# Preparing a seven-product pair's weights beside the two chunks in front of it, with the plain blocks' high parts in a tile of the large pool

## Chip, cores and metric

The kernel runs on one core of a Trainium2 chip. The metric is the device time of one execution in microseconds; before the change the median of three runs is 1595.82 us (1594.87 to 1597.53).

## What is computed

One decoder layer over 256 tokens of width 2048, all in float32:

```python
u = rmsnorm(h, g_mix);  proj = u @ w_in                    # q, k, v, z, xBC, dt, two gates
out_a = attention(q, k, v) @ w_attn_br                      # sliding window, sinks
out_s = rmsnorm(ssd(xBC, dt) * silu(z), g_ssd) @ w_ssd_br   # state-space mixer
h = h + (sigmoid(g_a) * out_a + sigmoid(g_s) * out_s) @ w_o
f = rmsnorm(h, g_ffn)
h = h + (silu(f @ w_gate) * (f @ w_up)) @ w_down            # hidden width 5632
h = h + sigmoid(rmsnorm(h, g_ple) @ w_ple_gate) * (p @ w_ple_proj)
out = rmsnorm(h, g_final)
```

Nearly all of the time goes into products of 256 tokens with weight matrices that are read once from HBM.

## The kernel before

**Products.** A float32 matrix is split into a high part (a cast to float32r) and a low part (what the cast left). A product is three matmuls: high with high, high with low, low with high, each of 128 rows, 128 tokens and 512 columns. For weights, ScalarE (ACT) makes the high part `wh` from the loaded tile `wr`, and VectorE (DVE) makes the low part `wl` as `wr - wh`.

**Wide blocks.** `wide_block` computes 256 tokens by two column halves (q = 0, 1) of 512. It walks over pairs `kp` of 128-row slices of the weights. A plain pair is two chunks, one for each column half: a chunk is one load of 512 KB on SyncE's (SP's) queue (L298), one cast (L309), one subtraction (L311) and 4 products, that is 12 matmuls, written at L249. The last products of one pair are followed by the first of the next; only TensorE's (PE's) sums in PSUM link them.

**Seven-product pairs.** For the pairs named in `forms` a scheme of Strassen's kind makes 7 products (21 matmuls) of what would be 8 (24). It needs the two loads `raw[0]`, `raw[1]`, four additions of weight blocks into `tr` (L329; each 128x512, the last two each need the one ahead), and splits (L337 on ACT, L338 on DVE) of three plain blocks, b11 and b21 (one 128x1024 cast and subtraction) and b22 (128x512), and of `tr` (128x2048, parts `th` and `tl`). Products are taken in the order q1 (b11), c11 (b21), c12 (b22), q6, q7, q5, c21 (the four sums). There are 40 such pairs: 22 in the eleven blocks of `hidden` (the gate and up weights; pairs 2 and 5 of eight), 10 with `w_down`, 4 with the gate of the second branch, 2 with `w_ssd_br`, 2 with `w_o`. Two of them are never neighbours.

**Buffers.** `wr` has 4 buffers, `wh` 4, `wl` 3; the pool `big` has 17 buffers of 8 KB per partition for everything large. A `wl` tile is free again when PE has done the chunk that reads it. A seven-product pair takes 2 of `wr`, 2 of `wh`, 2 of `wl` (one for b22 alone) and 3 of `big` (`tr`, `th`, `tl`).

**Order.** Every engine executes its instructions in an order fixed when the kernel is built. The tile framework draws it up: among the instructions that it holds to be ready, the one that stands first in the source goes first, so the source's order is a preference and not the order itself. Work of other stages (transposes, normalisation sums) waits in a queue, of which `pump` writes out one or two items after each chunk.

Around a block's start DVE also has the end of the block before: `settle` (L361), the gated product (L1062) in `hidden`, or `add_settled` (L365, L367), and the splits of transposed activations (L133, L139).

Of the kernel before, what the change touches and what calls it, by code (L numbers as in the profile page):

```python
# [11 lines left out]
F32 = mybir.dt.float32  # L12
F32R = mybir.dt.float32r
I32 = mybir.dt.int32
AF = mybir.ActivationFunctionType
ALU = mybir.AluOpType
AX = mybir.AxisListType

P = 128
# [4 lines left out]
NB = 512  # L24
# [37 lines left out]
def block_kernel(ctx: ExitStack, tc: tile.TileContext, x, x_t, p_t, positions, vecs, rows, g_final,  # L62
                 w_in, w_attn_br, w_ssd_br, w_o, w_gate, w_up, w_down, w_ple_gate,
                 w_ple_proj, out):
    nc = tc.nc
# [3 lines left out]
    wraw_p = ctx.enter_context(tc.tile_pool(name="wraw", bufs=4))  # L69
    whi_p = ctx.enter_context(tc.tile_pool(name="whi", bufs=4))  # L70
    wlo_p = ctx.enter_context(tc.tile_pool(name="wlo", bufs=3))
# [5 lines left out]
    def big(shape, dtype=F32, name="big"):  # L77
        return big_p.tile(shape, dtype, name=name, tag="big")
# [18 lines left out]
    def pump(n):  # L97
        for _ in range(n):
            for q in (side, heads):
                if q:  # L100
                    q.popleft()()
# [57 lines left out]
    def stat(tiles, k):  # L159
        return tiles[k // 4][:, 0, k % 4, :], tiles[k // 4][:, 1, k % 4, :]  # L160
# [120 lines left out]
    def wide_block(halves, lhs, nk, forms, pumps=1):  # L281

        psum.reverse()
        np_, ns = nk // 2, len(forms)  # L290
        c11, c12, c21, c22 = sums = [
            Sums(acc_tile, 2 * (np_ - ns) + (ns if i < 3 else 0)) for i in range(4)]
        shared, done = None, 0
        parts = [None] * 4

        def load(q, kp, dst):
            w, col0 = halves[q]
            nc.sync.dma_start(out=dst, in_=w[2 * kp * P:2 * (kp + 1) * P, col0:col0 + NB].rearrange(  # L298
                "(k p) n -> p k n", p=P))

        for kp in range(np_):
            ev, od = lhs(2 * kp), lhs(2 * kp + 1)
            tok = [[[x[:, t * P:(t + 1) * P] for x in k] for k in (ev, od)] for t in range(NT)]
            if kp not in forms:
                for q in range(2):
                    wr = wraw_p.tile([P, 2, NB], F32, name="wr", tag="wr")
                    load(q, kp, wr)
                    wh = whi_p.tile([P, 2, NB], F32R, name="wh", tag="wh")
                    nc.scalar.copy(out=wh, in_=wr)  # L309
                    wl = wlo_p.tile([P, 2, NB], F32R, name="wl", tag="wl")  # L310
                    nc.vector.tensor_tensor(out=wl, in0=wr, in1=wh.bitcast(F32), op=ALU.subtract)  # L311
                    for k in range(2):
                        for t in range(NT):
                            sums[2 * t + q].add(tok[t][k], (wh[:, k], wl[:, k]))
                    pump(pumps)
                continue
            if shared is None:
                shared = [Sums(aux_tile, ns) for _ in range(4)]
            q1, q5, q6, q7 = shared
            a, g2, f3, s3 = [[forms[kp][:, i, 0], forms[kp][:, i, 1]] for i in range(4)]  # L320
            raw = [wraw_p.tile([P, 2, NB], F32, name="wr", tag="wr") for _ in range(2)]
            for q in range(2):
                load(q, kp, raw[q])
            tr = big([P, 4, NB], F32, name="tr")
            for o, x, y in ((tr[:, 0], raw[0][:, 0], raw[1][:, 0]),
                            (tr[:, 1], raw[1][:, 0], raw[1][:, 1]),
                            (tr[:, 2], tr[:, 1], raw[0][:, 0]),
                            (tr[:, 3], tr[:, 2], raw[0][:, 1])):
                nc.vector.tensor_tensor(out=o, in0=x, in1=y, op=ALU.add)  # L329
            split = []  # L330
            for x, xh, xl in (
                    (raw[0], whi_p.tile([P, 2, NB], F32R, name="wh", tag="wh"),
                     wlo_p.tile([P, 2, NB], F32R, name="wl", tag="wl")),
                    (raw[1][:, 1:2], whi_p.tile([P, 2, NB], F32R, name="wh", tag="wh")[:, 1:2],
                     wlo_p.tile([P, 2, NB], F32R, name="wl", tag="wl")[:, 1:2]),
                    (tr, big([P, 4, NB], F32R, name="th"), big([P, 4, NB], F32R, name="tl"))):
                nc.scalar.copy(out=xh, in_=x)  # L337
                nc.vector.tensor_tensor(out=xl, in0=x, in1=xh.bitcast(F32), op=ALU.subtract)  # L338
                split.extend((xh[:, i], xl[:, i]) for i in range(x.shape[1]))
            b11, b21, b22, t1, t3, t2, t4 = split  # L340
            q1.add(tok[0][0], b11)
            c11.add(tok[0][1], b21)
            c12.add(f3, b22)
            q6.add(g2, t2)
            q7.add(s3, t3)
            q5.add(a, t1)
            c21.add(tok[1][1], t4)
            pump(2 * pumps)
            done += 1
            if done == ns:  # L350
                mid = big([P, 4, NB], F32, name="mid")
                parts = [mid[:, i] for i in range(4)]
                nc.scalar.copy(out=parts[0], in_=q1.tile)
                for o, x, y, op in ((3, 0, q6, ALU.subtract), (2, 3, q7, ALU.add),
                                    (1, 3, q5, ALU.add), (3, 2, q5, ALU.add)):
                    nc.vector.tensor_tensor(out=parts[o], in0=parts[x], in1=y.tile, op=op)
        return [x.tile for x in sums], parts
# [248 lines left out]
    for t in range(NT):  # L606
        nc.vector.scalar_tensor_tensor(out=dtv[:, t], in0=accs[1][t][:, W2 - SSM_H:W2],
                                       scalar=r1[:, t:t + 1],
                                       in1=row[:, R_DTB:R_DTB + SSM_H],
# [354 lines left out]
    def cols(j):  # L964
        return slice(j * NB, (j + 1) * NB)
# [19 lines left out]
    for j in range(4):  # L985
        accs = nblock(w_attn_br, j * NB, lambda k: stat(attnT, k), 8)
        for t in range(NT):
            nc.vector.tensor_tensor(out=merged[t][:, cols(j)], in0=accs[0][t],
                                    in1=merged[t][:, cols(j)], op=ALU.mult)
# [17 lines left out]
    for jj in range(2):  # L1007
        sums, parts = wide_block(column_pair(w_in, GSO, jj), lhs_u, KD, uforms)
        for i in range(4):
            settle(i, sums, parts)  # L1010
            nc.scalar.activation(out=parts[i], in_=parts[i], func=AF.Sigmoid,
                                 scale=r1[:, i // 2:i // 2 + 1])
        gates.append(parts)
    mforms = form_tiles((5,), "mforms")
    for jj in range(2):
        sums, parts = wide_block(column_pair(w_ssd_br, 0, jj), lambda k: stat(yT, k), KD, yforms)
        for i in range(4):
            t, c = i // 2, cols(2 * jj + i % 2)
            settle(i, sums, parts)
            nc.vector.scalar_tensor_tensor(out=parts[i], in0=parts[i], scalar=r2[:, t:t + 1],  # L1020
                                           in1=gates[jj][i], op0=ALU.mult, op1=ALU.mult)
            nc.vector.tensor_tensor(out=merged[t][:, c], in0=merged[t][:, c], in1=parts[i],
                                    op=ALU.add)
        for q in range(2):
            queue_flip(merged, mergedT, 2 * jj + q, None, mforms)
# [19 lines left out]
    for jj in range(2):  # L1045
        add_to_h(jj, *wide_block(column_pair(w_o, 0, jj), lambda k: stat(mergedT, k), KD, mforms))
        for q in range(2):
            queue_flip(h, hT, 2 * jj + q, V_GFFN, hforms)
            side.append(lambda j=2 * jj + q: square_sum(j, ssq3))
# [127 lines left out]
    def step(piece, k, wh, wl):  # L1177
        t, c0, n = pieces[piece]
        hi, lo = stat(h2T, k)
        ts, cs = slice(t * P, (t + 1) * P), slice(c0, c0 + n)  # L1180
        nc.tensor.matmul(outs[piece], hi[:, ts], wh[:, cs], start=(k == 0), stop=False)
        nc.tensor.matmul(outs[piece], hi[:, ts], wl[:, cs], start=False, stop=False)
        nc.tensor.matmul(outs[piece], lo[:, ts], wh[:, cs], start=False, stop=(k == KD - 1))

    for c in range(KD // 4):
        wr = wraw_p.tile([P, 2, NB], F32, name="wr", tag="wr")
        nc.sync.dma_start(out=wr, in_=w_ple_gate[2 * c * P:2 * (c + 1) * P, 3 * NB:].rearrange(
            "(k p) n -> p k n", p=P))
        wh = whi_p.tile([P, 2, NB], F32R, name="wh", tag="wh")
        nc.scalar.copy(out=wh, in_=wr)  # L1190
        wl = wlo_p.tile([P, 2, NB], F32R, name="wl", tag="wl")
# [73 lines left out]
```

## Time and profile before

| | |
|---|---|
| median of 3 runs | 1595.82 us |
| profiled execution | 1594.49 us, span 1592.8 us |
| TensorE matmul, busy share of the span | 99% |
| TensorE weight load | 82% |
| VectorE | 75% |
| ScalarE | 53% |
| granted TensorE clock | 0.998 of full speed |
| read from HBM | 293 MB, 185 GB/s over the span |

A busy share says how much of the span an engine executed something. Matmuls are pipelined, so the records of two neighbours overlap and a busy PE can still lose time; what it loses is seen in the distance between the starts of neighbouring matmuls.

### The profile page before, as it was taken

The page shows a single profiled execution, that of the slowest core. Times are in us where ns is not written, and L with a number is a line of the kernel's source. Part 1 is how long each engine was busy: PE and PEld are TensorE (multiplying, and loading weights), DVE is VectorE, ACT ScalarE, POOL GpSimd, SP SyncE. Part 2 cuts the span into 40 slices and gives each one's busy share as a digit, 9 for nine tenths or more (in the row PEclk, how much of TensorE's full clock was granted, in tenths as well). Part 3 has the DMA queues.
Part 4 walks back from the last instruction along what each step waited for, and adds up shares of the span by engine and source line. Part 5 has one row for each costly group of instructions (what it writes and reads, how often), then busy time and mean ns, then how long its engine had stood idle before and what let it go on. Part 6 is the DMA issues. An engine that isn't in the chain of part 4 may idle for free.

```text
span 1592.8 us, 19985 instructions
## 1 busy us (share of the span) xinstructions
PE 1574.0 (99%) x7298; PEld 1300.5 (82%) x7298; DVE 1201.3 (75%) x1507; ACT 844.2 (53%) x1073; POOL 132.1 (8%) x136
## 2 busy tenths in 40 slices
PE   9999999999999999999999999999999999999997
PEld 7988888888888888788788888788888878888886
DVE  8776766666666768788888788887878788788874
ACT  6654665555644554445655554455545444556653
POOL 1014224143210000000000000000000000000000
PEclk9999999999999999999999999999999999999999
DMA  8666435555646666655566655566665566655672
GB/s 270 177 198 185 136 105 158 158 161 157 178 157 183 210 199 213 209 195 189 173 199 195 198 188 197 185 210 193 193 196 177 194 203 199 220 189 185 200 228 87
DMA packets 152562, 296.63 MB, mean 186 GB/s; under 512 B 9536, under 2 KB 9664, under 8 KB 152080
## 3 DMA queue, kind: packets, MB, share of 16 engines
q1 hardware_dynamic: 151168, 290.76, 58.3%
q0 software_dynamic: 576, 3.47, 0.7%
q8 instruction: 57, 0.93, 0.2%
q10 hardware_dynamic: 720, 1.14, 0.2%
q14 instruction: 41, 0.34, 0.1%
HBM read 293.23 MB, written 2.10 MB: 185 GB/s over the span
## 4 chain that ended last, share of the span: by engine, by line
PE 92%; DVE 2%; DMA 2%; ACT 2%; issue 1%; POOL 0%; POOLq 0%; DVEq 0%; SPq 0%; ACTq 0%
PE aux L249 29%; PE acc L249 27%; PE acc L204 9%; PE acc L206 9%; PE acc L205 9%; PE aux L150 1%; DMA wr<-in_w_in_dram 1%; PE aux L754 1%; DMA wr<-in_w_gate_dram 1%; ACT th L337 1%; PE acc L150 1%; DVE tl L338 1%; PE aux L935 1%; PE aux L693 0%; ACT sc L899 0%
## 5 line engine op out<-in xcount | busy, mean ns | idle before, releaser
L309 ACT CAST wh<-wr 128x1024 fp32r<-128x1024 f32 x280 | 293.6, 1053 | 269.4 <-PE acc L249 97.2
L311 DVE TENSOR_TENSOR wl<-wr,wh 128x1024 fp32r<-128x1024 f32 x280 | 337.3, 1221 | 88.2 <-issue 35.8
L195 DVE TENSOR_TENSOR wl<-wr,wh 128x1024 fp32r<-128x1024 f32 (+1 forms) x172 | 227.6, 1330 | 119.6 <-PE acc L205 87.4
L193 ACT CAST wh<-wr 128x1024 fp32r<-128x1024 f32 (+1 forms) x172 | 173.7, 1013 | 167.9 <-PE acc L206 125.6
L249 PE MATMUL aux<-wh,flipT 128*128 128x512 f32 x736 | 237.8, 392 | 0.0
L249 PE MATMUL acc<-wh,flipT 128*128 128x512 f32 x640 | 208.4, 393 | 0.0
L204 PE MATMUL acc<-wh,uT 128*128 128x512 f32 (+1 forms) x512 | 200.3, 391 | 0.7 <-ACT cb L481 0.7
L206 PE MATMUL acc<-wh,uT 128*128 128x512 f32 (+1 forms) x512 | 194.2, 379 | 0.0
L205 PE MATMUL acc<-wl,uT 128*128 128x512 f32 (+1 forms) x512 | 193.9, 379 | 0.0
L249 PEld LDWEIGHTS aux<-wh,flipT 128*128 128x128 f32 x736 | 138.1, 188 | 28.3
L249 PE MATMUL aux<-wl,flipT 128*128 128x512 f32 x368 | 143.8, 391 | 0.6 <-DVE wl L311 0.6
L337 ACT CAST wh<-wr 128x1024 fp32r<-128x1024 f32 x80 | 66.8, 837 | 140.2 <-PE aux L249 62.4
L249 PEld LDWEIGHTS acc<-wh,flipT 128*128 128x128 f32 x640 | 120.2, 188 | 24.6 <-ACT wh L337 0.2
L249 PE MATMUL acc<-wl,flipT 128*128 128x512 f32 x320 | 124.6, 389 | 0.0
L338 DVE TENSOR_TENSOR tl<-tr,th 128x2048 fp32r<-128x2048 f32 x40 | 91.7, 2292 | 26.2 <-ACT th L337 26.1
L204 PEld LDWEIGHTS acc<-wh,uT 128*128 128x128 f32 x512 | 96.3, 188 | 18.1 <-issue 1.4
L205 PEld LDWEIGHTS acc<-wl,uT 128*128 128x128 f32 x512 | 96.4, 188 | 17.6 <-issue 1.0
L206 PEld LDWEIGHTS acc<-wh,uT 128*128 128x128 f32 x512 | 96.2, 188 | 17.8
L337 ACT CAST th<-tr 128x2048 fp32r<-128x2048 f32 x40 | 76.5, 1911 | 51.7 <-DVE tr L329 51.7
L249 PE MATMUL aux<-wh,actT 128*128 128x512 f32 x292 | 95.3, 393 | 0.0
L249 PE MATMUL acc<-wh,actT 128*128 128x512 f32 x292 | 93.6, 390 | 0.0
L338 DVE TENSOR_TENSOR wl<-wr,wh 128x1024 fp32r<-128x1024 f32 x80 | 76.2, 954 | 7.8 <-PE aux L249 4.0
(476 smaller groups left out, 2741.4 us busy)
## 6 DMA issues: line engine op xcount, KB each, us to landing
wr<-in_w_in_dram SPq DMA_DIRECT2D x144, 512.0 KB, 3.7
wr<-in_w_gate_dram SPq DMA_DIRECT2D x88, 512.0 KB, 3.7
wr<-in_w_up_dram SPq DMA_DIRECT2D x88, 512.0 KB, 4.1
wr<-in_w_down_dram SPq DMA_DIRECT2D x88, 512.0 KB, 4.4
wr<-in_w_ssd_br_dram SPq DMA_DIRECT2D x32, 512.0 KB, 4.3
wr<-in_w_o_dram SPq DMA_DIRECT2D x32, 512.0 KB, 4.0
wr<-in_w_ple_gate_dram SPq DMA_DIRECT2D x32, 512.0 KB, 4.9
wr<-in_w_in_dram SPq DMA_DIRECT2D x32, 256.0 KB, 3.9
```

The costliest lines, as they stand in the source:

```text
L150: nc.tensor.transpose(out=ps[:, j, t * P:(t + 1) * P], in_=src[t][:, c:c + P], identity=ident)
L193: nc.scalar.copy(out=wh, in_=wr)
L195: nc.vector.tensor_tensor(out=wl, in0=wr, in1=wh.bitcast(F32), op=ALU.subtract)
L204: nc.tensor.matmul(o, hi[:, ts], wh[:, kk, cs], start=(k == 0), stop=False)
L205: nc.tensor.matmul(o, hi[:, ts], wl[:, kk, cs], start=False, stop=False)
L206: nc.tensor.matmul(o, lo[:, ts], wh[:, kk, cs], start=False, stop=(k == nk - 1))
L249: nc.tensor.matmul(self.tile, a, b, start=self.first, stop=self.left == 0)
L309: nc.scalar.copy(out=wh, in_=wr)
L311: nc.vector.tensor_tensor(out=wl, in0=wr, in1=wh.bitcast(F32), op=ALU.subtract)
L337: nc.scalar.copy(out=xh, in_=x)
L338: nc.vector.tensor_tensor(out=xl, in0=x, in1=xh.bitcast(F32), op=ALU.subtract)
L754: nc.tensor.matmul(ps[:, es], m[:, t, e, :], xd[:, t, 0, es], start=True, stop=True)
```

## The change

`wide_block` gets a generator `prepared(kp)` for a seven-product pair and a helper `step(kp)` that runs it one step further. In the plain pair in front of a seven-product pair, the chunk of column half 0 calls it after its own load (the two loads of the coming pair are issued) and after its products (additions, and splits of b11, b21, b22); the chunk of column half 1 calls it after its products (split of `tr`). The pair itself only takes what is ready. The high parts of b11, b21 and b22 and the low part of b22 lie in one new tile `sh` of the pool `big`; the low parts of b11 and b21 stay in one `wl` tile. So a pair takes 2 of `wr`, none of `wh`, 1 of `wl` and 4 of `big`. Loads, additions, casts, subtractions and matmuls are the same in number and shape.

```diff
+        def prepared(kp):
+            raw = [wraw_p.tile([P, 2, NB], F32, name="wr", tag="wr") for _ in range(2)]
+            for q in range(2):
+                load(q, kp, raw[q])
+            yield
+            tr = big([P, 4, NB], F32, name="tr")
+            for o, x, y in (...):
+                nc.vector.tensor_tensor(out=o, in0=x, in1=y, op=ALU.add)
+            sh = big([P, 4, NB], F32R, name="sh")
+            wl = wlo_p.tile([P, 2, NB], F32R, name="wl", tag="wl")
+            split = []
+            def part(x, xh, xl):
+                nc.scalar.copy(out=xh, in_=x)
+                nc.vector.tensor_tensor(out=xl, in0=x, in1=xh.bitcast(F32), op=ALU.subtract)
+                split.extend((xh[:, i], xl[:, i]) for i in range(x.shape[1]))
+            part(raw[0], sh[:, 0:2], wl)
+            part(raw[1][:, 1:2], sh[:, 2:3], sh[:, 3:4])
+            yield
+            part(tr, big([P, 4, NB], F32R, name="th"), big([P, 4, NB], F32R, name="tl"))
+            yield
+            yield split
...
                     load(q, kp, wr)
+                    if q == 0:
+                        step(kp + 1)
                     wh = whi_p.tile([P, 2, NB], F32R, name="wh", tag="wh")
...
                             sums[2 * t + q].add(tok[t][k], (wh[:, k], wl[:, k]))
+                    step(kp + 1)
                     pump(pumps)
                 continue
...
-            raw = [wraw_p.tile([P, 2, NB], F32, name="wr", tag="wr") for _ in range(2)]
-            for q in range(2):
-                load(q, kp, raw[q])
-            tr = big([P, 4, NB], F32, name="tr")
...
-            b11, b21, b22, t1, t3, t2, t4 = split
+            b11, b21, b22, t1, t3, t2, t4 = step(kp)
```

## Rows read from the trace of the kernel before

**Rows 1.** The page's head and section 1: busy time, share, instructions.
```profile
span 1592.8 us, 19985 instructions
PE 1574.0 (99%) x7298; PEld 1300.5 (82%) x7298; DVE 1201.3 (75%) x1507; ACT 844.2 (53%) x1073; POOL 132.1 (8%) x136
```

**Rows 2.** The chain that ended last, in order of time (start, us, what).
```profile
959.87 11.56 PE aux L249 x51
```

**Rows 3.** Waits of PE's weight loads (waiter, releaser: us in total, times, longest).
```profile
PEld acc L249 <- DVE wl L338: 4.9, 3, 2.1
PEld aux L249 <- DVE tl L338: 3.0, 7, 0.7
PEld acc L249 <- DVE tl L338: 2.4, 5, 1.1
PEld aux L249 <- DVE wl L311: 2.0, 4, 1.0
...
PEld aux L249 <- DVE wl L338: 0.8, 2, 0.6
```

**Rows 4.** Waits of PE's matmuls, same columns.
```profile
PE acc L249 <- DVE wl L338: 3.6, 3, 1.6
...
PE acc L249 <- DVE tl L338: 0.7, 1, 0.7
```

**Rows 5.** Timeline of PE, 1013.5 to 1017.5 us (start, us, what, idle before).
```profile
1015.21 0.39 PE L249 MATMUL acc<-wh,aforms 128*128 128x512 f32 x1
1016.25 0.50 PE L249 MATMUL acc<-wl,aforms 128*128 128x512 f32 x1 [0.66 <-DVE wl L338]
```

**Rows 6.** Timeline of DVE over the same pair, last pair of a w_down block.
```profile
1013.30 2.29 DVE L338 TENSOR_TENSOR tl<-tr,th 128x2048 fp32r<-128x2048 f32 x1 [0.84 <-ACT th L337]
1015.51 0.68 DVE L338 TENSOR_TENSOR wl<-wr,wh 128x512 fp32r<-128x512 f32 x1
```

**Rows 7.** Timeline of PE where `tl` came late, block of hidden after w_down.
```profile
1299.87 0.39 PE L249 MATMUL aux<-wl,flipT 128*128 128x512 f32 x1
1300.93 0.50 PE L249 MATMUL acc<-tl,hforms 128*128 128x512 f32 x1 [0.67 <-DVE tl L338]
```

**Rows 8.** Timeline of DVE in mid-block, 1301 to 1315 us, second pair of hidden.
```profile
1305.17 1.23 DVE L311 TENSOR_TENSOR wl<-wr,wh 128x1024 fp32r<-128x1024 f32 x1 [2.02 <-issue]
1306.31 1.29 DVE L329 TENSOR_TENSOR tr<-wr 128x512 f32<-128x512 f32 x2
...
1308.25 1.22 DVE L338 TENSOR_TENSOR wl<-wr,wh 128x1024 fp32r<-128x1024 f32 x1
```

**Rows 9.** Timeline of DVE from a regular hidden block's start to its first pair.
```profile
1323.53 1.23 DVE L311 TENSOR_TENSOR wl<-wr,wh 128x1024 fp32r<-128x1024 f32 x1 [1.49 <-PE aux L249]
...
1332.12 1.22 DVE L311 TENSOR_TENSOR wl<-wr,wh 128x1024 fp32r<-128x1024 f32 x1
1333.26 0.69 DVE L329 TENSOR_TENSOR tr<-wr 128x512 f32<-128x512 f32 x1
1333.86 0.69 DVE L133 TENSOR_TENSOR actT<-aux,actT 128x512 fp32r<-128x512 f32 x1
```

**Rows 10.** Timeline of PE in the same block.
```profile
1338.31 0.39 PE L249 MATMUL acc<-wl,flipT 128*128 128x512 f32 x1
...
1343.98 0.39 PE L249 MATMUL acc<-wl,flipT 128*128 128x512 f32 x1
1344.32 0.50 PE L249 MATMUL aux<-tl,hforms 128*128 128x512 f32 x1
```

**Rows 11.** SP's loads in wide blocks: issues around that start, and landing.
```profile
1324.78 0.37 SPq L298 DMA_DIRECT2D wr<-in_w_gate_dram  x1
...
DMA to landing us min/median/max: 3.5/3.9/7.7
```

**Rows 12.** Timeline of DVE at the first hidden block, after w_o.
```profile
775.13 1.22 DVE L311 TENSOR_TENSOR wl<-wr,wh 128x1024 fp32r<-128x1024 f32 x1
...
776.66 1.28 DVE L329 TENSOR_TENSOR tr<-wr 128x512 f32<-128x512 f32 x2
```

More of the change, by code (lines that the diff above doesn't have):

```diff
@@ L299, in load, with step @@
                 "(k p) n -> p k n", p=P))
+        def prepared(kp):
[4 more added lines that the diff above has]
+            tr = big([P, 4, NB], F32, name="tr")
+            for o, x, y in ((tr[:, 0], raw[0][:, 0], raw[1][:, 0]),
+                            (tr[:, 1], raw[1][:, 0], raw[1][:, 1]),
+                            (tr[:, 2], tr[:, 1], raw[0][:, 0]),
+                            (tr[:, 3], tr[:, 2], raw[0][:, 1])):
+                nc.vector.tensor_tensor(out=o, in0=x, in1=y, op=ALU.add)
[12 more added lines that the diff above has]
+            yield split
+        ready = {}
+        def step(kp):
+            if kp in forms:
+                if kp not in ready:
+                    ready[kp] = prepared(kp)
+                return next(ready[kp])
         for kp in range(np_):
@@ L320, in wide_block @@
             a, g2, f3, s3 = [[forms[kp][:, i, 0], forms[kp][:, i, 1]] for i in range(4)]
-            raw = [wraw_p.tile([P, 2, NB], F32, name="wr", tag="wr") for _ in range(2)]
-            for q in range(2):
-                load(q, kp, raw[q])
-            tr = big([P, 4, NB], F32, name="tr")
[L325 to L339, printed above, removed]
-            b11, b21, b22, t1, t3, t2, t4 = split
+            b11, b21, b22, t1, t3, t2, t4 = step(kp)
             q1.add(tok[0][0], b11)
```

## The prediction, made before the changed kernel ran

> **What bounds the kernel now.** Read the page's head first [rows 1]: PE 99% busy, VectorE 75%, one core at nearly full clock. Busy time of pipelined matmuls proves little, so the next view is the chain that ended last: 51 matmuls in 11.56 us, one every 0.227 us [rows 2]. That is PE's pace when nothing is late, and a seven-product pair (21 matmuls) is 4.76 us of it, a chunk (12) 2.72 us, a plain pair 5.44 us. The change leaves the number of matmuls alone, so it can only win back the places where PE falls out of this pace. The waits of PE's weight loads say where these are [rows 3]: 5.7 us in 5 waits on L338's `wl` (4.9 + 0.8), 5.4 us in 12 waits on L338's `tl` (3.0 + 2.4), and 2.0 us on the plain chunks' L311. Everything that the change aims at is in the first two, 11.1 us; the waits of the matmuls themselves put it far lower, at 3.6 + 0.7 = 4.3 us [rows 4]. Neither is the loss: a weight load goes ahead of its matmul, so its wait is too long, and the record of a matmul is longer than its pace, so its idle time is too short. The loss is the distance of starts less 0.227 us. For one wait it is 1016.25 - 1015.21 - 0.23 = 0.81 us where the row says 0.66 [rows 5], for another 1300.93 - 1299.87 - 0.23 = 0.83 us [rows 7] where the longest wait of a weight load on `tl` is 1.1 us [rows 3], so about three quarters of that view.
>
> A rule speaks against this reading: the Trainium skill (Perfetto Trace Analysis, section Identifying the Most-Contended Engine) judges TensorE's headroom by the busy share of weight loads and not of matmuls. By that rule 18% of the span, some 290 us, would be open; the trace doesn't agree, as starts 0.227 us apart leave none of it [rows 2].
>
> **The late low part of b22.** The rows show how it arises [rows 6]: in the last pair before a block ends DVE does `tl` (1013.30, 2.29 us) and only then the low part of b22 (1015.51), because that tile is the pair's second of the three `wl` buffers and has to wait until PE has left the chunk that holds it. PE asks for it 1.4 us into the pair and stands still. The change puts it in `sh`, in the large pool, and its subtraction in front of PE's arrival by a whole chunk. Three such waits cost 3.6 us by PE's idle time and 4.9 us by the weight load's [rows 3, 4]; with 0.15 us more each than the idle time, as above, 4.1 us. The two short ones (0.8 us) add 0.6. Gain 4.7 us (bounds 3.6 to 5.7).
>
> **The late `tl`.** The same DVE and ACT work ends about a chunk earlier, so the twelve waits go: 5.4 us times three quarters, 4.1 us (bounds 0.7 by PE's idle time, 5.4). What is late next is below.
>
> **What is moved, and past what.** Nothing is added in count. Per pair, DVE has four additions, the subtractions of 1.22, 0.69 and 2.29 us [rows 6, 8]: all of it now stands in front of, or between, the two subtractions of the plain pair. On SP's queue the pair's two loads go ahead of the load of the chunk of column half 1, which therefore takes the `wr` buffer that comes free two chunks later. Before, a load is issued when the `wl` four chunks back is done, and lands 3.9 us later in the median, 7.7 at most [rows 11]; two chunks are 5.4 us. In mid-block a chunk's `wl` ends about 4.1 us ahead of its use (the buffer comes free as PE starts the chunk two in front, 5.44 us, less 1.23 us; its waits on PE [rows 9] are this), so that load is issued some 4.1 + 5.4 us before its use: 3.9 us of landing, cast and subtraction fit. I price it at nothing in mid-block; a landing of 7.7 us would take the cover away, at 0.4 us or so for such a load. POOL's queue isn't passed. `big` needs 4 tiles per pair, not 3: by the source at most 12 lie there for long in a w_down block, so 16, and `mid` is the 17th of 17; as `tr` is dead by then I price this at nothing too (a wait there would hold `mid` and the block's end, below 1 us each).
>
> **The chunk of column half 1 now waits behind the pair.** VectorE has one order. After the plain pair's first `wl`, it has to do four additions, b11/b21, b22, and only then the second `wl`. Successive starts lie closer than durations: two additions in about 1.2 us [rows 8] and one each 0.6 [rows 9]; the dependent two take some 0.7 each. So 2.6 + 1.14 + 0.61 + 1.22 = 5.6 us from the end of one `wl` to the end of the next. PE needs the second 2.72 us after the first, and the first is 4.1 us early: 6.8 us. In mid-block [rows 8] that is 1.2 us to spare: nothing lost in 29 pairs (upper bound 0.2 us each, 6 us, if every such chunk came late as `tl` does now).
>
> At the start of a `hidden` block there is no such lead, since DVE first ends the block before. The rows give it [rows 9]: DVE is through with that at 1332.12, where the second `wl` of pair 1 now starts. After the change the additions come there: 2.6 us, two splits of transposed activations in the middle (L133, 0.6 each), 1.14 + 0.61 for the pair, 5.6 us in all, then the second `wl`, 1337.7 to 1338.9. PE wants it at 1338.31 [rows 10]: 0.6 us late, 1.1 if durations and not starts are summed. Against that, where `tl` was late in this very block, PE had other products in between and lost only 1344.32 - 1343.98 - 0.23 = 0.11 us, twice [rows 10]: the order drawn up at build time fills a lateness that it foresees. So between 0 and 1.1 us for each of eleven blocks. I take 0.4, between 0.22 where PE was given other work and 0.6 where not: 4.4 us (0 to 12.1).
>
> The Trainium skill says that VectorE, ScalarE and GpSimd take their instructions strictly first in, first out (Perfetto Trace Analysis, section Tensor Engine Instruction). By that rule the case at the 1.1 us end, the rival below, is the one to fear; rows 6 agree, where a ready engine does b22 after `tl`.
>
> **Sum.** Against the profiled execution, 1594.49 us: -4.7 - 4.1 + 4.4 = -4.4, so 1590.1 us. Its own time lies 1.3 us below the median of the runs; carried over, 1591.4 us.
>
> **Rivals.** *The loss only changes its place.* DVE's work per pair is the same, and what was late in the pair is late one chunk sooner: 11 blocks at 0.8 us are 8.8 us against 8.8 us won. For it speaks that DVE has no room at a block's start [rows 9], against it that the largest waits lie at a block's end [rows 5, 6]. It gives 1595.8 us, with 1593 to 1599 for 0.5 to 1.1 us a block.
>
> *Slower: the second `wl` of pair 1 in `hidden`.* The place is the chunk of column half 1 in front of pair 2, eleven times. Price 1.1 us each, 12.1 us, if the order of PE was drawn up in the belief that this `wl` comes in time. And of the gains only PE's idle time is won, 4.3 us. That gives 1595.8 + 12.1 - 4.3 = 1603.6 us. It decides from 0.8 us a block on if all gains come, from 0.4 if only the small ones do. For it: the three waits on b22 [rows 4] are just such a misjudged order. Against it: the same block's `tl` shows a well judged one.
>
> *The change doesn't do what it says.* The source's order is a preference. In the first `hidden` block a later chunk's L311 (775.13) goes ahead of the pair's additions (776.66) [rows 12]. If additions and loads keep their old places, only b22's buffer is new: 4.7 us won, nothing lost, 1591.1 us, hardly told from my forecast by the time alone.
>
> **How the numbers follow.** Forecast 0.49 (1587.0 with all gains of 8.8 us and no new loss, to 1592.6), loss displaced 0.27, slower 0.18, order kept 0.06. The likeliest gives 1591.4 us. The range reaches from 1586.0, between 1587.0 and the 1584.7 us that the weight loads' waits would give (11.1 us won), to 1601.0, and leaves out some 0.03 below and 0.12 of the slower rival's upper part. A measurement of this kernel can tell about 0.2%, 3.2 us, from no change. Faster by more is below 1592.6: the forecast, the order kept, less 0.03 for its upper edge, 0.52. Slower by more is above 1599.0: 0.18. Within: 0.30.
>
> **What would show each step.** The waits on L338's `wl` should be gone in the waits of PE and its weight loads, and most on `tl`. In the timeline of `hidden` DVE should do `tr` before the second `wl` of pair 1, and a wait of PE on L311 there, times eleven, is the term of 4.4 us: at 0 the kernel is near 1587, at 1.1 near 1599. Loads of the coming pair should stand on SP ahead of the second load of the pair in front. The prediction is wrong if waits on DMA take the place of those on DVE (the 7.7 us landing), if PE's pace itself differs from 0.227 us, or if `mid` or `tr` waits for a buffer.

## The result: 1612.7 us, slower by 1.0%, and the profile after

The changed kernel takes 1612.72 us (median of four runs, 1612.08 to 1613.37), the kernel before 1596.18 us beside it: a ratio of 1.0104, 95% interval 1.0086 to 1.0121. The forecast was 1591.4 us with a range up to 1601.0: wrong in sign and outside the range.

The page of the changed kernel, head and section 1 (busy us, share of the span, instructions), for [rows 1]:

```profile
span 1610.4 us, 19876 instructions
PE 1579.7 (98%) x7298; PEld 1303.5 (81%) x7298; DVE 1203.9 (75%) x1507; ACT 845.3 (52%) x1073; POOL 132.1 (8%) x136
```

The work is the same, the span 17.6 us longer. The waits of PE's weight loads (PEld) and matmuls on the wide blocks' line, for [rows 3, 4] (waiter, releaser: us in total, times, longest):

```profile
PEld acc L249 <- DVE wl L350: 12.1, 11, 4.6
PE acc L249 <- DVE wl L350: 8.4, 6, 4.2
PEld aux L249 <- DVE wl L350: 5.2, 6, 2.2
PEld acc L249 <- ACT sh L319: 3.7, 2, 1.9
PEld acc L249 <- DVE wl L320: 3.3, 2, 1.7
PE acc L249 <- ACT sh L319: 2.9, 2, 1.5
PE acc L249 <- DVE wl L320: 2.4, 2, 1.2
PE aux L249 <- DVE wl L350: 2.4, 3, 1.7
```

What the change aimed at is gone: PE waits neither for `tl` nor for b22's low part. In their place stand plain chunks (L350, the old L311), 17.3 us of PEld's waits where there were 2.3 (2.0 of it in [rows 3]), and the pair's own high part and its subtraction (L319, L320), 3.7 and 3.3 us. Few waits make it up, the longest 4.6 us.

Where they lie is told by the loss that the prediction defines, the distance of the starts of neighbouring matmuls less 0.227 us, summed over each of the 23 wide blocks in the trace (distances less than 0.012 us over that left out). Each row is one profiled execution, which lies up to 4 us from its kernel's median (e2 3.9 us below, e12 2.9 us above), so blocks are compared here and not small differences of sums. Blocks are counted from 0: "SSD 1" is the second block with `w_ssd_br`, "w_down 1.0" the first block of `w_down`'s first third.

| loss in us | SSD 1 | w_o 0 | hidden 0 | hidden 2 | hidden 4 | hidden 6 | hidden 8 | w_down 1.1 | w_down 2.1 | all 23 |
|---|---|---|---|---|---|---|---|---|---|---|
| before | 2.4 | 0.4 | 1.5 | 0.4 | 0.5 | 0.3 | 1.2 | 1.3 | 2.2 | 15.2 |
| changed | 7.8 | 2.5 | 0.6 | 6.3 | 0.0 | 5.4 | 0.0 | 1.6 | 1.9 | 31.5 |
| e1, tile alone | 3.2 | 0.4 | 5.1 | 3.7 | 5.0 | 4.5 | 6.8 | 1.5 | 1.3 | 37.5 |
| e2, second load first | 6.0 | 0.6 | 1.6 | 5.1 | 1.6 | 5.3 | 1.7 | 2.1 | 1.2 | 31.1 |
| e3, second `wl` first | 3.1 | 0.4 | 1.5 | 4.3 | 1.0 | 3.1 | 0.0 | 1.9 | 0.0 | 19.8 |
| e4, forms later | 8.4 | 2.4 | 0.7 | 0.4 | 0.0 | 0.4 | 0.0 | 2.3 | 2.1 | 21.6 |
| e5, low tile alone | 2.7 | 0.4 | 1.9 | 0.5 | 1.6 | 0.9 | 1.6 | 0.6 | 1.0 | 15.7 |
| e6, moved, highs in `wh` | 4.3 | 0.6 | 0.7 | 1.8 | 0.0 | 1.7 | 0.0 | 0.6 | 1.1 | 15.2 |
| e7 = e3 + e4 | 3.2 | 0.5 | 1.0 | 0.6 | 0.0 | 0.3 | 0.0 | 0.0 | 0.0 | 10.3 |
| e9, forms' tile granted early | 8.3 | 0.4 | 0.6 | 0.3 | 0.0 | 0.4 | 0.2 | 4.2 | 1.4 | 21.1 |
| e12 = e7 + `h` later | 0.8 | 0.5 | 1.5 | 0.4 | 1.0 | 1.2 | 0.0 | 1.5 | 0.0 | 11.7 |

Of the 17.6 us, 16.3 are in the last column: 11.1 in hidden 2 and 6, 5.4 in SSD 1, 2.0 in w_o 0, 1.6 in two blocks not shown (the first with `w_ssd_br` and the first of `w_down`'s last third), less 3.8 won elsewhere. Each of the large places has one stall, or two close together. Here is hidden 2 in four stretches (busy time and count of PE, PEld, DVE, ACT, POOL, then granted clock, DMA share, GB/s):

```profile
860.00:866.00 6.00, 6.00 (x31) 4.81 (x30) 3.76 (x6) 2.59 (x3) 0.00 (x0) 1.00 0.52 170
866.00:873.00 7.00, 4.34 (x21) 2.97 (x18) 5.49 (x11) 3.44 (x7) 0.00 (x0) 0.93 0.00 0
873.00:879.00 6.00, 6.00 (x14) 4.38 (x15) 6.00 (x6) 3.18 (x3) 0.00 (x0) 0.51 0.74 243
879.00:885.00 6.00, 6.00 (x28) 4.94 (x27) 3.95 (x5) 3.55 (x4) 0.00 (x0) 1.00 0.90 280
```

From 866 to 873 PE runs dry and DMA moves nothing, as all four `wr` buffers are held. Then PE is called busy throughout but starts 14 matmuls in 6 us where the next 6 us hold 28: the granted clock is 0.51, the lower of its two levels, 1.2 GHz. So about half of this block's loss is the standstill and half is what follows it.

Why PE ran dry is read from ScalarE, VectorE and PE in the same place (start, us, engine, line, what, idle before and its releaser):

```profile
862.31 1.05 ACT L348 CAST wh<-wr 128x1024 fp32r<-128x1024 f32 x1 [2.52 <-DMA wr<-in_w_up_dram]
...
869.38 0.62 ACT L277 CAST aforms<-fm 128x512 fp32r<-128x512 f32 x1 [1.01 <-DVE fm L276]
869.91 1.56 ACT L319 CAST sh<-wr 128x1024 fp32r<-128x1024 f32 x2
```
```profile
869.27 1.29 DVE L312 TENSOR_TENSOR tr<-wr 128x512 f32<-128x512 f32 x2
...
871.68 1.22 DVE L320 TENSOR_TENSOR wl<-wr,sh 128x1024 fp32r<-128x1024 f32 x1
...
874.02 2.35 DVE L350 TENSOR_TENSOR wl<-wr,wh 128x1024 fp32r<-128x1024 f32 x2
```
```profile
871.00 0.50 PE L249 MATMUL acc<-sh,flipT 128*128 128x512 f32 x1 [1.44 <-ACT sh L319]
...
872.95 0.80 PE L249 MATMUL acc<-wl,flipT 128*128 128x512 f32 x1 [1.22 <-DVE wl L320]
873.54 0.63 PE L249 MATMUL acc<-sh,flipT 128*128 128x512 f32 x1
873.97 0.63 PE L249 MATMUL aux<-wl,flipT 128*128 128x512 f32 x1
874.40 0.63 PE L249 MATMUL aux<-sh,flipT 128*128 128x512 f32 x1
```

The second chunk's cast is through at 863.36, and its weights would be ready a microsecond or so later. But its subtraction is done at 874.02, behind the pair's (871.68), which needs the cast to `sh` (869.91), which comes right after the first write to `aforms` (869.38), the token forms (the sums of activations that a seven-product pair multiplies with) of a pair of `w_down` that is wanted much later. What PE itself stands for here, as in hidden 6, is the pair: PE's order has the pair's first products ahead of what reads the second chunk's `wl`, so its waits are on `sh` (1.44 us) and on the pair's `wl` (1.22 us). The pair's loads were issued at 852.90 and 855.64: its data are not what is late. The last rows show the low clock as distances of 0.43 us. The Trainium skill (TensorE: Matmul & The Clock Gate, section Wait — 56ns, not 53.3ns?) gives 426.7 ns for 512 columns at the lower clock, with which these rows agree, and 215.7 ns at the full one, which this kernel does not reach: its pace there is 0.227 us.

In SSD 1 the form is another. DVE, PE, and the stretch that follows:

```profile
656.82 2.29 DVE L320 TENSOR_TENSOR tl<-tr,th 128x2048 fp32r<-128x2048 f32 x1 [0.84 <-ACT th L319]
659.02 2.36 DVE L350 TENSOR_TENSOR wl<-wr,wh 128x1024 fp32r<-128x1024 f32 x2
```
```profile
660.30 0.72 PE L249 MATMUL acc<-wl,yT 128*128 128x512 f32 x1 [4.15 <-DVE wl L350]
```
```profile
660.20:664.20 4.00, 3.90 (x10) 3.08 (x11) 1.18 (x2) 1.05 (x1) 0.00 (x0) 0.57 0.59 197
```

The second chunk's cast starts at 653.51 and ends a microsecond later; VectorE does `tl`, which is needed after it, first. Then again the low clock, 0.57. w_o 0 has the same order at 707.46.

One thing more has moved in SSD 1. The two loads of `h` (1 MB each, for tiles of the large pool) were issued 17 us apart before; now they come together, in this block (GpSimd, POOL, in the kernel before and in the changed one):

```profile
616.18 0.60 POOL L1030 DMA_DIRECT2D h<-in_x_dram  x1 [152.56 <-PE aux L249]
633.17 0.54 POOL L1030 DMA_DIRECT2D h<-in_x_dram  x1 [16.38 <-DVE mid L1020]
```
```profile
634.49 0.60 POOL L1051 DMA_DIRECT2D h<-in_x_dram  x1 [169.93 <-PE aux L150]
635.66 0.54 POOL L1051 DMA_DIRECT2D h<-in_x_dram  x1 [0.57 <-DVE merged L1043]
```

### The profile page after: what moved, and what is told of

It reads as the page before. It is cut to its first block, busy times and chain, and to the rows that moved or that the text cites. A ratio compares the mean times of both kernels' runs of the same rounds, so it can differ in the third digit from the quotient of the medians.

```text
span 1610.4 us, 19876 instructions
## 1 busy us (share of the span) xinstructions
PE 1579.7 (98%) x7298; PEld 1303.5 (81%) x7298; DVE 1203.9 (75%) x1507; ACT 845.3 (52%) x1073; POOL 132.1 (8%) x136
## 4 chain that ended last, share of the span: by engine, by line
PE 93%; DVE 2%; DMA 2%; ACT 1%; issue 1%; POOL 0%; POOLq 0%; DVEq 0%; SPq 0%; ACTq 0%
PE aux L249 30%; PE acc L249 28%; PE acc L204 9%; PE acc L206 9%; PE acc L205 9%; DMA wr<-in_w_in_dram 1%; PE aux L150 1%; DVE wl L350 1%; PE aux L775 1%; PE acc L150 1%; DMA wr<-in_w_ssd_br_dram 1%; PE aux L956 1%; PE aux L714 0%; ACT sc L920 0%; PE aux L902 0%
## 5 line engine op out<-in xcount | busy, mean ns | idle before, releaser
L348 ACT CAST wh<-wr 128x1024 fp32r<-128x1024 f32 x280 | 294.6, 1053 | 417.7 <-PE acc L249 114.2
L350 DVE TENSOR_TENSOR wl<-wr,wh 128x1024 fp32r<-128x1024 f32 x280 | 339.2, 1222 | 98.9 <-PE aux L249 37.7
L249 PE MATMUL aux<-wh,flipT 128*128 128x512 f32 x688 | 220.7, 394 | 0.0
L249 PE MATMUL acc<-wh,flipT 128*128 128x512 f32 x592 | 189.6, 393 | 0.0
L249 PEld LDWEIGHTS aux<-wh,flipT 128*128 128x128 f32 x688 | 130.4, 190 | 26.9
L249 PEld LDWEIGHTS acc<-wh,flipT 128*128 128x128 f32 x592 | 111.2, 188 | 22.6
L205 PEld LDWEIGHTS acc<-wl,uT 128*128 128x128 f32 x512 | 96.3, 188 | 17.6 <-issue 1.0
L320 DVE TENSOR_TENSOR tl<-tr,th 128x2048 fp32r<-128x2048 f32 x40 | 91.6, 2290 | 25.1 <-ACT th L319 25.1
L249 PE MATMUL aux<-wh,actT 128*128 128x512 f32 x272 | 87.5, 393 | 0.0
L319 ACT CAST th<-tr 128x2048 fp32r<-128x2048 f32 x40 | 76.4, 1909 | 19.6 <-DVE tr L312 18.4
L249 PE MATMUL acc<-wh,actT 128*128 128x512 f32 x272 | 85.7, 390 | 0.0
L249 PEld LDWEIGHTS aux<-wl,flipT 128*128 128x128 f32 x368 | 70.1, 191 | 18.1 <-DVE wl L350 3.8
L319 ACT CAST sh<-wr 128x1024 fp32r<-128x1024 f32 x80 | 65.6, 836 | 27.6 <-DMA wr<-in_w_down_dram 11.8
```

Of the source, the lines that this page charges most:

```text
L205: nc.tensor.matmul(o, hi[:, ts], wl[:, kk, cs], start=False, stop=False)
L249: nc.tensor.matmul(self.tile, a, b, start=self.first, stop=self.left == 0)
```

## Experiments

**The parts one by one: the tile and the move.** e1 keeps loads, additions and splits in their old place and takes over only the tile:

```diff
-                    if q == 0:
-                        step(kp + 1)
...
-                    step(kp + 1)
                     pump(pumps)
...
-            b11, b21, b22, t1, t3, t2, t4 = step(kp)
+            b11, b21, b22, t1, t3, t2, t4 = [step(kp) for _ in range(4)][3]
```

> One part of the change alone: the pair's weights are loaded, added and split where the kernel before does it (after the plain pair), but the high parts lie in the tile sh of the pool big and b22's low part too. Theory (the loss comes from the pair's work and loads standing ahead of the second chunk of the pair in front, the tile is harmless): the waits on b22's low part go and no new loss comes, 1590 to 1594 us, with the blocks SSD 1 and hidden 2 and 6 at their losses of before (2.4, 0.4, 0.3 us). Rival (the tile in the large pool is the cause, through its buffers): 1608 us or more, with these three blocks losing 5 to 8 us each.

Measured: 1615.78 us, 1.0121 of before (1.0104 to 1.0138). The rival's side: the tile alone costs more than the whole change. But of the blocks that it named each loses only 3.2 to 4.5 us; hidden 0, 4 and 8 lose more, 5.0 to 6.8 us. ScalarE and PE in hidden 4:

```profile
1043.87 1.05 ACT L346 CAST wh<-wr 128x1024 fp32r<-128x1024 f32 x1 [3.10 <-DMA wr<-in_w_gate_dram]
1045.17 1.06 ACT L346 CAST wh<-wr 128x1024 fp32r<-128x1024 f32 x1 [0.25 <-DMA wr<-in_w_up_dram]
1046.12 1.90 ACT L319 CAST th<-tr 128x2048 fp32r<-128x2048 f32 x1
```
```profile
1048.07 0.49 PE L249 MATMUL acc<-th,hforms 128*128 128x512 f32 x1 [1.04 <-ACT th L319]
1050.40 0.50 PE L249 MATMUL acc<-tl,hforms 128*128 128x512 f32 x1 [1.83 <-DVE tl L320]
```

The additions end at 1043.97, but two plain casts of the chunks after the pair, the second waiting for its load, stand ahead of `th`. As the pair takes no `wh` buffers any more, nothing held these casts back when the order was drawn up. That reading is tested by putting the high parts back into `wh`: e5 with everything in the old place, e6 with everything moved as in the change. In both b22's low part has a tile of its own in the large pool.

```diff
-            sh = big([P, 4, NB], F32R, name="sh")
+            sh = big([P, 1, NB], F32R, name="sh")
+            wh0, wh1 = [whi_p.tile([P, 2, NB], F32R, name="wh", tag="wh") for _ in range(2)]
...
-            part(raw[0], sh[:, 0:2], wl)
-            part(raw[1][:, 1:2], sh[:, 2:3], sh[:, 3:4])
+            part(raw[0], wh0, wl)
+            part(raw[1][:, 1:2], wh1[:, 1:2], sh)
```

> The kernel before with one edit: the low part of b22 gets a tile of its own in the large pool; the high parts stay in wh, everything stays in its place. Theory (in the run with the tile alone, the wh buffers that the pair no longer takes let ScalarE's fixed order put two plain casts ahead of th, and these wait for loads; so th and tl come late and PE stands still and runs at the low clock afterwards): with the high parts back in wh the casts stay behind th, only the waits on b22's low part go, 1590 to 1594 us, and hidden 0, 2, 4, 6 and 8 lose at most 1.5 us each. Rival (the low part's place in the large pool is the cause): 1605 to 1616 us.

Measured: 1595.42 us, 1.0000 (0.9990 to 1.0010), a little above the theory's range. Hidden 0, 4 and 8 lose 1.6 to 1.9 us, just over the bound given, and far less than in e1, so the high parts' place is the cause of e1's loss and the low part's is not. But the low part's place wins nothing either: the waits on it are all but gone, and hidden 4, 6, 8 and 10 lose 0.3 to 1.1 us more. This run, like e6, takes four tiles of the large pool for a pair, as the changed kernel does, so their number is not what costs. It did move `h`: the first load is issued at 633.03 here and the second at 634.21. By itself that costs little, as SSD 1 loses 2.7 us.

> The changed kernel (loads, additions and splits moved ahead) with the high parts in wh as before and only b22's low part in the large pool. Theory (forms ahead of the additions cost hidden 2 and 6 whatever the wh buffers do; the loads' order costs SSD 1 and w_o): 1598 to 1608 us, hidden 2 and 6 above 3 us each. Rival (the freed wh buffers are the whole cause of the loss): 1588 to 1595 us.

Measured: 1596.68 us, 1.0013 (1.0003 to 1.0022): a miss for the theory, which had the forms cost over 3 us in hidden 2 and 6 whatever the buffers do, where they lose 1.8 and 1.7; the time lies between its range and the rival's. The four runs form a square: high parts in `wh`, 1.0000 in the old place and 1.0013 moved; in `sh`, 1.0121 and 1.0104. The move by itself is worth next to nothing either way; the high parts in the large pool cost 1.2% and 0.9%, 19 and 15 us. In hidden 2 of e6 the order is this (ACT, then DVE):

```profile
853.70 1.06 ACT L320 CAST wh<-wr 128x1024 fp32r<-128x1024 f32 x1 [0.26 <-PE acc L249]
```
```profile
856.64 1.22 DVE L321 TENSOR_TENSOR wl<-wr,wh 128x1024 fp32r<-128x1024 f32 x1
...
860.71 1.23 DVE L351 TENSOR_TENSOR wl<-wr,wh 128x1024 fp32r<-128x1024 f32 x1 [1.89 <-ACT wh L349]
```

The pair's cast starts 7 us after its load is issued (846.58), not 17 us, and both subtractions are done before the forms (`fm` at 862.99) and the additions (864.12), which are as late as before.

**Why `sh` waits for `aforms`.** Two edits on the changed kernel. e4 makes these token forms ten items later in the side queue, from the split parts (one addition more):

```diff
         for i in range(2):
             side.append(lambda i=i: transpose_pair(act, i * 2 * P, dst, 2 * i, None,
-                                                   forms.get(kp0 + i)))
+                                                   None if kp0 + i == 3 else forms.get(kp0 + i)))
+        if kp0 == 2 and 3 in forms:
+            side.extend((idle,) * 10)
+            side.append(lambda: token_forms(joined(kept, 3), forms[3]))
```

> The changed kernel with the token forms of w_down's pair 3 made ten items later in the queue of side work, so that they do not stand ahead of the pair's additions in hidden 2 and 6; everything else as changed. Theory (in these two blocks VectorE's fixed order holds the additions behind the forms, and so the second chunk behind both): both blocks fall from 6.3 and 5.4 us to below 1 us, 1600 to 1604 us. Rival (any block whose pair work stands ahead of the second chunk loses when loads are slow, forms or not): 1609 to 1614 us, both blocks still above 4 us.

Measured: 1603.60 us, 1.0044 (1.0029 to 1.0058); both blocks at 0.4 us. e9 leaves the forms where they are and adds one small write to every tile of token forms where it is allocated:

```diff
         tile = big([P, 2, 4, 2, P], F32R, name=name)
+        nc.gpsimd.memset(tile[:, 0, 0, 0, 0:1].bitcast(F32), 0.0)
```

> The changed kernel with one small write more: GpSimd sets one column of each tile of token forms when that tile is allocated. Nothing else moves in the source; the forms' own work stays where it stood. Theory (buffers of the large pool are given out in the source's order of first writes, so the casts to sh and the additions to tr of hidden 2 and 6 had to wait until the forms ahead of them were written): both blocks fall below 1 us, 1600 to 1604 us. Rival (VectorE's work on the forms itself, or its place in the source, is what delays them): both stay above 4 us, 1610 to 1614 us.

Measured: 1600.53 us, 1.0028 (1.0016 to 1.0040), both blocks at 0.3 and 0.4 us. Hidden 2 of this run, ACT, DVE and a stretch with PE's clock:

```profile
862.95 1.57 ACT L319 CAST sh<-wr 128x1024 fp32r<-128x1024 f32 x2
...
866.75 0.66 ACT L256 ACTIVATE fsc<-acc 128x256 f32<-128x256 f32 x2 [0.80 <-DVE actT L133]
```
```profile
861.58 0.69 DVE L312 TENSOR_TENSOR tr<-wr 128x512 f32<-128x512 f32 x1
...
868.45 1.22 DVE L350 TENSOR_TENSOR wl<-wr,wh 128x1024 fp32r<-128x1024 f32 x1
```
```profile
868.00:874.00 6.00, 6.00 (x28) 4.79 (x27) 6.00 (x8) 3.41 (x4) 0.00 (x0) 1.00 0.76 261
```

The forms' work is all there, and the cast to `sh` now goes ahead of it: 11.0 us of these two blocks' loss come back for a write of one column. So it was neither VectorE's time nor the number of buffers. The reading that fits both runs: a buffer of a pool is given out when the first write to its tile is due, and tiles are served in the source's order of first writes; a tile that waits for late data holds up all that stand behind it. The `wl` tiles show the same: of the 353 that the changed kernel writes after 490 us none is written ahead of one that precedes it in the source. That is the second link of the chain in hidden 2: the second chunk's `wl` comes after the pair's `wl`, and that after `sh`.

The early write is made to every forms' tile, and other blocks change too. w_o 0 falls to 0.4 us, since VectorE now does the second chunk's subtraction ahead of `tl`:

```profile
705.64 1.22 DVE L350 TENSOR_TENSOR wl<-wr,wh 128x1024 fp32r<-128x1024 f32 x1
708.82 2.29 DVE L320 TENSOR_TENSOR tl<-tr,th 128x2048 fp32r<-128x2048 f32 x1 [1.96 <-ACT th L319]
```

w_down 1.1 rises by 2.6 us; there the subtraction stands behind `tl`, as in the changed kernel, and PE waits 2.29 us for it where it waited 1.31. SSD 1 stays high, at 8.3 us.

**SSD 1 and w_o 0.** e2 puts the load of the second chunk back ahead of the pair's two; e3 leaves the loads and writes additions and splits behind the second chunk's subtraction.

```diff
# e2
+                wrs = [wraw_p.tile([P, 2, NB], F32, name="wr", tag="wr") for _ in range(2)]
+                for q in range(2):
+                    load(q, kp, wrs[q])
+                step(kp + 1)
                 for q in range(2):
-                    wr = wraw_p.tile([P, 2, NB], F32, name="wr", tag="wr")
-                    load(q, kp, wr)
-                    if q == 0:
-                        step(kp + 1)
+                    wr = wrs[q]
# e3
                     nc.vector.tensor_tensor(out=wl, in0=wr, in1=wh.bitcast(F32), op=ALU.subtract)
+                    if q == 1:
+                        step(kp + 1)
...
-                    step(kp + 1)
+                    if q == 1:
+                        step(kp + 1)
                     pump(pumps)
```

> The changed kernel with the load of the chunk of column half 1 back ahead of the pair's two loads; additions and splits stay ahead of that chunk's subtraction. Theory (in SSD 1, w_o and the ends of w_down the second chunk's load is late, so the build-time order puts its subtraction behind tl; in hidden 2 and 6 it is the token forms, whatever the loads do): the first group's 8 us come back and the 11 us of hidden 2 and 6 stay, 1602 to 1606 us. Rival (VectorE's place for the additions alone is the cause): 1611 to 1614 us. Rival (the loads' order is the whole cause): 1591 to 1597 us.

Measured: 1614.78 us, 1.0111 (1.0094 to 1.0129). This is above all three ranges and nearest to the first rival. The loads' order is not it, but for w_o 0, which falls to 0.6 us. SSD 1 stays at 6.0.

> The changed kernel with the additions and splits written behind the second chunk's subtraction, its load still behind the pair's two loads. Theory (the load's place decides, as the source is only a preference and the second chunk's weights are there late): most of the loss stays, 1606 to 1614 us, hidden 2 and 6 among it. Rival (the additions' place in the source is the cause): 1591 to 1598 us.

Measured: 1597.14 us, 1.0009 (0.9998 to 1.0020); the rival, within its upper bound. SSD 1 falls to 3.1 us and w_o 0 to 0.4, hidden 2 and 6 stay at 4.3 and 3.1, as the tiles behind `aforms` must. DVE in SSD 1, with the second chunk's subtraction (cast from 651.73) now ahead of `tl`, and the stretch that had the low clock:

```profile
652.87 1.22 DVE L350 TENSOR_TENSOR wl<-wr,wh 128x1024 fp32r<-128x1024 f32 x1
654.94 2.29 DVE L320 TENSOR_TENSOR tl<-tr,th 128x2048 fp32r<-128x2048 f32 x1 [0.85 <-ACT th L319]
```
```profile
660.20:664.20 4.00, 4.00 (x19) 3.32 (x18) 1.57 (x2) 0.00 (x0) 0.00 (x0) 1.00 0.92 286
```

e10 takes away the other suspect, the 2 MB of `h` that come over GpSimd's queue in this block (7.4 and 9.3 us to landing):

```diff
-    h = [big([P, D], F32, name="h") for _ in range(NT)]
-    for t in range(NT):
-        nc.gpsimd.dma_start(out=h[t], in_=x[t * P:(t + 1) * P, :])
+    h = []
+    def load_h(t):
+        h.append(big([P, D], F32, name="h"))
+        nc.gpsimd.dma_start(out=h[t], in_=x[t * P:(t + 1) * P, :])
+    side.extend(lambda t=t: load_h(t) for t in range(NT))
```

> The changed kernel with the two 1 MB loads of h, on GpSimd's queue, moved from the end of the second branch into w_o's first block. Theory (in SSD 1 these loads slow the weights', and this alone makes the second chunk late): SSD 1 falls from 7.8 to below 2.5 us, 1605 to 1608 us. Rival (the fixed order, tl ahead of the second chunk's subtraction, costs that much without them too): SSD 1 stays above 5 us, 1611 to 1614 us.

Measured: 1610.43 us, 1.0087 (1.0071 to 1.0104), between the two. SSD 1 falls from 7.8 to 4.3 us, w_o 0 rises from 2.5 to 4.3, with the loads issued at 652.4 and 656.1, behind those of the pair in question. In SSD 1 `tl` still goes ahead of the second chunk's subtraction, and PE now waits 1.98 us for it instead of 4.15 (DVE, then PE):

```profile
655.75 2.35 DVE L350 TENSOR_TENSOR wl<-wr,wh 128x1024 fp32r<-128x1024 f32 x2
```
```profile
657.02 0.50 PE L249 MATMUL acc<-wl,yT 128*128 128x512 f32 x1 [1.98 <-DVE wl L350]
```

So two causes overlap in SSD 1. Of the 5.4 us more than before, moving `h` takes back 3.5 and the new order alone 4.8 (e3, with `h` where it was); the two shares can't simply be added.

**Together.** e7 is e3 and e4 at once, e12 adds e10's edit, e11 is e3 with early writes for the tiles of forms and of transposed activations, e8 has e2's, e3's, e4's and e6's edits.

> The changed kernel with two edits at once: additions and splits behind the second chunk's subtraction, and the token forms of w_down's pair 3 later in the side queue. Theory (the two causes add up: what is left of the loss with the first edit alone lies in hidden 2 and 6, 4.3 and 3.1 us, of which some 0.4 each stay): 1590 to 1592.5 us. Rival (the loss moves on to other blocks): 1595 to 1600 us.

Measured: 1592.43 us, 0.9982 (0.9972 to 0.9991). The causes add up, and here gains of the forecast's size do come: w_down 1.1 and 2.1, hidden 4 and 8 lose nothing, where before they lost 5.2 us.

> The run with the second chunk's subtraction first and the forms later (1592.4 us), and the loads of h moved into w_o's first block. Theory (SSD 1's 3.2 us come from h's loads): 1588.5 to 1590.5 us. Rival (they collide with w_o's loads there and cost as much): 1591.5 to 1594 us.

Measured: 1589.56 us, 0.9961 (0.9947 to 0.9974), faster than both kernels; SSD 1 falls from e7's 3.2 to 0.8 us. PE's matmuls wait on the wide blocks' weights only here and there:

```profile
PE acc L249 <- DVE tl L320: 1.2, 2, 0.7
...
PE acc L249 <- DVE wl L350: 0.8, 1, 0.8
```

> The run with the second chunk's subtraction ahead of the additions (1597.1 us), and the early small write for the tiles of forms and of transposed activations. Theory (what was left there, 4.3 and 3.1 us in hidden 2 and 6, is the same wait for a buffer given out in order): 1590 to 1592.5 us. Rival (it is the forms' work): 1595 to 1599 us.

Measured: 1600.08 us, 1.0031 (1.0018 to 1.0045), a miss. Hidden 2 and 6 fall to 1.5 and 1.1 us, but `tl` is now late in seven of the eleven hidden blocks (with 3.2 us lost in hidden 0, 1.0 in 1, 1.3 in 5, 2.0 in 10). That the early write to the tiles of activations changed the engines' order there is likely, but no run takes it by itself.

> All edits at once: the second chunk's load ahead of the pair's two, its subtraction ahead of the additions, token forms of w_down's pair 3 later, high parts in wh, only b22's low part in the large pool. Theory (each cause taken away; the waits on b22 and most on tl are won): 1586 to 1591.5 us, faster than the kernel before. Rival (the gain is used up elsewhere): 1594 to 1598 us.

Measured: 1594.17 us, 0.9992 (0.9982 to 1.0001), a miss. With the high parts in `wh` and the second chunk first, 15.1 us of loss remain, 2.8 us in SSD 1 and 1.3 to 2.1 us each in w_down 1.1, hidden 4, 8 and 10: the gain is used up elsewhere, as its rival said.

## Why the prediction was wrong

*PE's pace and the headroom.* Right: the loss by distances of starts accounts for 16.3 of 17.6 us, at the pace of 0.227 us.

*The late low part of b22, 4.7 us, and the late `tl`, 4.1 us.* The waits went as said, the gain did not stay. Hidden 0, 4, 8 and the second branch's first gate block won 3.1 us (some 0.8 of it a wait on a plain chunk, in hidden 0), while in w_down 1.1 and 2.1 the stall only moved from b22 to the second chunk: 3.5 us before and after, as in the rival of a loss that changes its place. In SSD 1, the third place with a long wait on b22, it grew. e5 shows it for b22 alone, 0.0%. e7 shows that such a gain can be had.

*The second `wl` of pair 1 in `hidden`, 4.4 us.* Wrong, and with it the slower rival's place. In an ordinary hidden block (hidden 9) DVE does the second `wl` behind the pair's additions and plain splits, as worked out, but PE has been given the pair's products in between (DVE, then PE):

```profile
1354.78 0.69 DVE L320 TENSOR_TENSOR sh<-wr,sh 128x512 fp32r<-128x512 f32 x1
1355.38 2.36 DVE L350 TENSOR_TENSOR wl<-wr,wh 128x1024 fp32r<-128x1024 f32 x2
```
```profile
1355.55 0.39 PE L249 MATMUL aux<-sh,flipT 128*128 128x512 f32 x1
...
1356.46 0.69 PE L249 MATMUL acc<-wl,flipT 128*128 128x512 f32 x2
```

Nothing is lost there, and the six ordinary blocks are 0.1 us faster each. In SSD 1 and w_o 0 the mechanism is that of the slower rival all the same, in other blocks than it named: PE's order asks for a second chunk's subtraction that comes later, and it costs 5.4 and 2.0 us more there, not 1.1. In hidden 2 and 6 it is neither, as PE waits for the pair itself.

*The step that failed* is the one that priced the large pool at nothing: "`big` needs 4 tiles per pair, not 3". I counted buffers. What counted was whose buffer is given out before whose, and which casts the four `wh` buffers had held back. The prediction's own sign, that `tr` waits for a buffer, came in hidden 2: its additions stand behind the forms there (869.27) and ahead of them in e9 (861.58). Moving the high parts into the pool costs 15 us with the move and 19 us without. In hidden 2 and 6 the cause is shown (e9): 11.1 of the 16.3 us. In SSD 1 and w_o 0, 7.5 us more than before, e3's new order takes back 6.8 us, and with `h` moved SSD 1 loses 3.5 us less (e10). Why the order was drawn up that way with `sh` and not with `wh` (w_o 0 at 0.6 us in e6) is argued only, from ScalarE's casts being free to go ahead; no run takes that by itself.

*Loads past each other on SyncE's queue, nothing.* Nearly right: e2 wins only w_o 0's 1.9 us and is no faster as a whole. But I had priced a slow landing at 0.4 us, and left out the loads of `h` on GpSimd's queue. That queue is not passed, but its first load moved from 616.18 to 634.49, beside the weights of SSD 1; e5, with the fourth tile of the large pool alone, has it at 633.03.

*What follows a stall.* The prediction valued a stall at its own length. In hidden 2, 14 starts in 6.00 us in place of 28 are some 3 us more on a standstill of 3.1 us.

## What to carry to other kernels

A tile that moves to another pool joins that pool's queue: ask not only whether a buffer is free but which tiles stand ahead of it in the source, and when their first write is due. Ask too what the old buffers were holding back, as a scarce pool can be what keeps an engine's fixed order sound. Where an order is drawn up at build time, make the work that is needed first stand first in the source, and price a stall of some microseconds at up to twice its length.

## What the runs showed of the hardware

After PE had stood for 4.2 us in SSD 1, the granted clock was 0.57 over the next 4 us; after its two waits of 1.4 and 1.2 us in hidden 2 it was 0.51 over 6 us. Starts were 0.43 us apart there, the lower level (1.2 GHz). Without the standstill, hidden 2 of e9 and SSD 1 of e3 have 1.00. Not every stall is followed by this: in SSD 1 of e6 PE waits 1.4 and 1.1 us within 3 us and the clock stays at 1.00 (652 to 664 us). Two loads of 1 MB on GpSimd's queue, issued 1.2 us apart, took 7.4 and 9.3 us to land, and a weight load issued at 639.17 beside them was waited for until 648.89.
